# Low parts of the GLU gate's and output gate's weight slabs: by VectorE, or by ScalarE and an adding DMA

## The chip, the core and the metric

One core of a Trainium2 chip runs the whole kernel in one launch. The metric is the device time in microseconds (us); the kernel before and the kernel after are compared on the same chip. The engines are named as in the profile: PE is TensorE, DVE is VectorE, ACT is ScalarE, POOL is GpSimd, and SP is SyncE, whose queue issues most DMAs.

## The reference

A trunk of two pre-norm residual layers and a final RMSNorm, over 512 positions of width 1024, in float32. The change lies in the first (even) layer:

```python
def even_layer(x, norm_g, w_in, w_uq, q_g, w_ukv, kv_g, conv_w, conv_b, ln_g, ln_b, w_out, cos, sin):
    u = rms_norm(x, norm_g) @ w_in
    q_c, kv_c, k_r, z_b, glu_a, glu_g, z_a = jnp.split(
        u, _offsets(Q_LORA, KV_LORA, QK_ROPE, MLA_W, CONV_W, CONV_W, CONV_W), axis=-1)
    o_b = mla(q_c, kv_c, k_r, w_uq, q_g, w_ukv, kv_g, cos, sin) * jax.nn.silu(z_b)
    o_a = conformer_conv(glu_a, glu_g, conv_w, conv_b, ln_g, ln_b) * jax.nn.silu(z_a)
    return x + (jnp.concatenate([o_b, o_a], axis=-1) @ w_out).astype(x.dtype)
```

`mla` is attention with 16 heads over low-rank queries and keys. `conformer_conv` forms `a * sigmoid(g)` (the GLU), then a depthwise convolution of width 31, a LayerNorm and a swish. The second (odd) layer has a Mamba-2 mixer and a short convolution.

## The kernel before

**Products in two parts.** PE multiplies in float32r. To reach float32's accuracy every operand is split into a high part (rounded to float32r) and a low part (the rest), and a product is three: high by high, high by low, low by high. A weight matrix comes in slabs of up to 128x1024 (8 k-tiles by 128 output channels), each of which gives one 128x512 tile of the result in 24 matmuls: 16 that read the high part `w_hi`, then 8 that read the low part `w_lo` (`mm_cm`, line L325 of the profile).

**The slabs.** `Weights` holds the list of all slabs in the order of their use. `_prepare` does one slab: it loads it from DRAM into `w_raw` (line L87, issued on SP's queue), casts it to `w_hi` on ACT (L91), and makes `w_lo` in one of two ways. For slabs whose key is in `BY_DMA` (all of the odd layer, save one) ACT writes minus the slab, rounded to float32r, into `w_lo` (L93), and a DMA that POOL issues adds `w_raw` to it in place (L94). For all others one subtraction `w_raw - w_hi` does it (L96): on DVE if the key is in `EARLY`, else on POOL, and the slabs of the output projections alternate between the two. There are two `w_raw` buffers and three each of `w_hi` and `w_lo` (the odd layer gets one more now and then). `next(key)` first prepares slabs until one slab beyond the asked one is ready (three beyond, for keys in `BY_DMA`), then hands one out. A counter `self.i` is raised at the head of `_prepare`, after the slab's entry was read.

**The order of the work.** The program only states what depends on what; a list scheduler at build time, with the program's order as priority and its own costs, writes one fixed queue for each engine. Each engine then runs its queue in order.

**The attention's loop.** It has eight passes (p = 0 to 7), each of two heads. A pass makes scores and exponentials (`probs`: PE, then the row maximum on DVE at L538, the exponential on ACT at L540), writes the inverse sums to DRAM and reads them back broadcast (`inverse`, L550 and L554, on SP's queue), makes the next keys (`uk` slabs), then a tile of the GLU (slabs `a` and `g`; in the last two passes two `za` slabs stand there instead), transposes the probabilities (`turn`: PE, then copies `pt` on ACT and DVE at L563), makes the output gate (slab `zb`, L359 and L360), and weighs the values (`weigh`, L573). After p = 1, 3 and 5 it also makes the next queries and values (`up_proj`, slabs `uq` and `uv`, copies `q_tm` at L510). Two tiles of the GLU are made ahead of the loop, with two `a` and two `g` slabs.

**The convolution.** `conv31` stands after the loop in the program, and the scheduler spreads it over the loop as work of low priority: 22 taps on DVE (L488), 8 side taps on POOL (L483 to L486), then ACT copies DVE's sum (`cs`, L490) and POOL adds both (`u`, L491). There is one buffer for the side taps and one for `cs`.

The list's order in the loop, by key:

```python
    for p in range(8):
        out += ["uk"] * (p < 7)
        out += (["a", "g"] if p < 6 else ["za", "za"]) + ["zb"]
        if p % 2 and p < 7:
            out.append("up%d" % ((p + 1) // 2))
```

Counted from one, slab 16 is the `a` of p = 0, slab 17 the first `g` in the loop; the two `g` ahead of it are slabs 8 and 10. Each "up" is three slabs (two `uq` and a `uv`).

Of the kernel before, what the change touches and what calls it, by code (L numbers as in the profile page):

```python
# [66 lines left out]
BY_DMA = ("C", "B", "x", "zc", "h", "gc", "gb", "zd")  # L67
# [3 lines left out]
class Weights:  # L71
# [7 lines left out]
    def _prepare(self):  # L79
        nc = self.tc.nc  # L80
        key, ap, kt, n = self.slabs[self.i]
        eng = nc.vector if key in EARLY or key in ("oe", "oo") and self.i % 2 else nc.gpsimd
        self.i += 1
        more = key in BY_DMA and self.i % 3 == 0
        raw = (self.more if more else self.pool).tile([P, D], F32, name="w_raw", tag="w_raw",
                                                      bufs=1 if more else self.raw_bufs)[:, :kt * n]
        nc.sync.dma_start(raw, ap)  # L87
        more = key in BY_DMA and self.i % 4 == 0
        hi, lo = ((self.more if more else self.pool).tile([P, D], F32R, name=nm, tag=nm, bufs=1 if more else self.bufs)
                  [:, :kt * n] for nm in ("w_hi", "w_lo"))  # L90
        nc.scalar.copy(hi, raw)  # L91
        if key in BY_DMA:
            nc.scalar.mul(lo, raw, -1.0)  # L93
            nc.gpsimd.dma_start(lo, raw, accum_op=ALU.add)  # L94
        else:
            eng.tensor_tensor(lo, raw, hi.bitcast(F32), op=ALU.subtract)  # L96
        v = lambda t: t.rearrange("p (k n) -> p k n", k=kt)
        self.ready.append((key, v(hi), v(lo)))
# [1060 lines left out]
```

## Time and profile before

| | |
|---|---|
| median of 3 runs | 958.86 us (955.78 to 959.15) |
| the profiled execution | 958.48 us |
| its span, first to last instruction | 956.7 us |
| mean granted clock of TensorE | 0.992 |
| PE, weight loads, DVE, ACT, POOL busy | 920.2, 741.1, 696.0, 507.7, 310.1 us |
| low parts by L96 on DVE | 74 slabs, 83.0 us |
| low parts by L96 on POOL | 20 slabs, 47.7 us |
| low parts by L93 and L94 | 45 slabs, 47.5 us on ACT, 39.2 us on POOL |

A row of the profile's groups reads: line, engine, operation, what it writes and reads, the shape of the first form, the count, then the busy time in us, the mean time of one in ns, and the idle time of the engine just before them with what ended it. A row of the timeline has the start in us from the span's first instruction, the duration in us, the engine, the line and the operation, and in brackets the idle time before it and its releaser. A row of the stretches has the busy time of PE, weight loads, DVE, ACT and POOL with the number of instructions, then the granted clock, the DMA engines' share and their GB/s.

### The profile page before, as it was taken

What the parts mean: (1) busy time and instruction counts of PE and PEld (TensorE: products, weight loads), DVE (VectorE), ACT (ScalarE), POOL (GpSimd) and SP (SyncE); (2) the same over time, 40 slices, a digit from 0 to 9 for tenths busy, and PEclk for the clock granted to TensorE, in tenths of its full rate; (3) what the DMA queues carried; (4) which work ended last, traced back from release to release, by engine and by line L of the source; (5) the groups of instructions that cost most, each with busy time, mean ns of one, the idle gap of its engine ahead of it and who ended that gap; (6) DMA issues with size and microseconds to landing.
All of it is one profiled execution on the core that took longest, in us unless ns stands there. A gap on an engine that the chain in (4) does not pass through costs nothing.

```text
span 956.7 us, 12593 instructions
## 1 busy us (share of the span) xinstructions
PE 920.2 (96%) x4528; PEld 741.1 (77%) x4528; DVE 696.0 (73%) x1292; ACT 507.7 (53%) x964; POOL 310.1 (32%) x269
## 2 busy tenths in 40 slices
PE   7899998999999999999999899999999999999996
PEld 7888686776877677888889578878786886888885
DVE  4699888999988999893163779777866886466315
ACT  6645454544554444373135487777667757444322
POOL 0142716347073443283222121121212222234222
PEclk9999999999999999999999899999999999999998
DMA  8303302212122215423347679868676776732222
GB/s 317 106 28 112 57 22 95 60 51 86 45 70 83 66 56 97 132 92 111 96 161 201 158 211 220 195 157 214 163 196 159 215 170 161 196 113 74 88 81 88
DMA packets 48373, 119.57 MB, mean 125 GB/s; under 512 B 12808, under 2 KB 14472, under 8 KB 48312
## 3 DMA queue, kind: packets, MB, share of 16 engines
q1 hardware_dynamic: 35304, 82.61, 26.7%
q0 software_dynamic: 6480, 23.60, 13.7%
q10 hardware_dynamic: 6528, 12.58, 4.4%
q8 instruction: 35, 0.57, 0.2%
q14 instruction: 26, 0.21, 0.1%
HBM read 90.85 MB, written 4.33 MB: 99 GB/s over the span
## 4 chain that ended last, share of the span: by engine, by line
PE 79%; DVE 13%; DMA 3%; ACT 3%; issue 1%; POOL 0%; SPq 0%; DVEq 0%; ACTq 0%; POOLq 0%
PE acc L325 39%; PE acc L352 10%; PE tp L352 5%; PE sb L352 5%; PE sb L536 5%; PE tp L273 5%; PE acc L573 3%; PE cv L352 3%; PE cv L945 2%; PE tp L961 1%; DMA sums_d<-sums 1%; ACT w_hi L91 1%; PE sb L273 1%; DVE w_lo L96 1%; DMA w_raw<-in_w_cm_o 1%
## 5 line engine op out<-in xcount | busy, mean ns | idle before, releaser
L325 PE MATMUL acc<-xT_hi,w_hi 128*128 128x512 f32 x616 | 249.2, 406 | 2.7 <-ACT xT_hi L413 2.7
L325 PE MATMUL acc<-xT_lo,w_hi 128*128 128x512 f32 x616 | 246.7, 401 | 0.1
L91 ACT CAST w_hi<-w_raw 128x1024 fp32r<-128x1024 f32 (+7 forms) x139 | 134.8, 971 | 200.8 <-PE acc L325 85.6
L325 PE MATMUL acc<-xT_hi,w_lo 128*128 128x512 f32 x616 | 155.1, 391 | 0.0
L96 DVE TENSOR_TENSOR w_lo<-w_raw,w_hi 128x1024 fp32r<-128x1024 f32 (+6 forms) x74 | 83.0, 1121 | 88.2 <-ACT w_hi L91 77.6
L325 PEld LDWEIGHTS acc<-xT_hi,w_hi 128*128 128x128 f32 x616 | 116.9, 190 | 27.3 <-ACT xT_hi L413 2.9
L488 DVE SCALAR_TENSOR_TENSOR cv<-u,pc,cv 128x497 f32<-128x497 f32 (+10 forms) x176 | 130.2, 740 | 10.1 <-ACT cv L477 7.7
L325 PEld LDWEIGHTS acc<-xT_lo,w_hi 128*128 128x128 f32 x616 | 116.8, 190 | 24.5 <-POOL xT_lo L414 0.8
L325 PEld LDWEIGHTS acc<-xT_hi,w_lo 128*128 128x128 f32 x616 | 115.4, 188 | 24.1
L94 POOL DMA_DIRECT2D w_lo<-w_raw x45 | 39.2, 871 | 180.5 <-ACT w_lo L93 128.2
L96 POOL TENSOR_TENSOR w_lo<-w_raw,w_hi 128x1024 fp32r<-128x1024 f32 (+1 forms) x20 | 47.7, 2387 | 112.0 <-ACT w_hi L91 104.2
L486 POOL TENSOR_TENSOR side<-side 128x510 f32<-128x510 f32 (+3 forms) x56 | 78.6, 1403 | 4.7
L491 POOL TENSOR_TENSOR u<-cs,side 128x512 f32<-128x512 f32 x8 | 11.0, 1375 | 157.1 <-issue 149.9
L540 ACT ACTIVATE p<-sb,mx 128x512 f32<-128x512 f32 x64 | 43.4, 683 | 20.8 <-DVE mx L538 20.5
L485 POOL TENSOR_SCALAR side<-u,pc 128x510 f32<-128x510 f32 (+3 forms) x56 | 50.2, 897 | 4.7
L93 ACT ACTIVATE w_lo<-w_raw 128x1024 fp32r<-128x1024 f32 x45 | 47.5, 1056 | 2.2 <-PE acc L325 2.2
L928 DVE SCALAR_TENSOR_TENSOR e<-e,nacs 128x128 f32<-128x128 f32 x96 | 30.1, 347 | 22.6 <-ACT e L927 22.5
L538 DVE TENSOR_REDUCE mx<-sb 128x1 f32<-128x512 f32 x64 | 41.7, 685 | 3.2 <-PE sb L536 2.6
L923 DVE SCALAR_TENSOR_TENSOR f<-cbm,dt,f 128x128 f32<-128x128 f32 x96 | 39.2, 444 | 5.6 <-ACT f L922 5.6
L273 PEld LDWEIGHTS tp<-kc,p 128*128 128x128 f32 x256 | 28.9, 140 | 16.1 <-ACT pt L563 10.7
L728 DVE SCALAR_TENSOR_TENSOR c<-acc,pc,c 128x510 f32<-128x510 f32 (+1 forms) x48 | 35.8, 745 | 6.3 <-ACT c L726 5.7
L536 PE MATMUL sb<-k_t,qk_hi 128*128 128x512 f32 (+1 forms) x128 | 39.5, 403 | 0.4 <-DVE k_t L264 0.4
(325 smaller groups left out, 1836.8 us busy)
## 6 DMA issues: line engine op xcount, KB each, us to landing
w_raw<-in_w_cm_o SPq DMA_DIRECT2D x45, 512.0 KB, 4.8
w_lo<-w_raw POOLq DMA_DIRECT2D x45, 512.0 KB, 5.9
w_raw<-in_w_cm_e SPq DMA_DIRECT2D x32, 512.0 KB, 3.5
e<-acs ACTq DMA_DIRECT2D x24, 512.0 KB, 6.0
w_raw<-in_w_out_e SPq DMA_DIRECT2D x16, 512.0 KB, 3.5
w_raw<-in_w_out_o SPq DMA_DIRECT2D x16, 512.0 KB, 3.3
xt<-in_xT SPq DMA_DIRECT2D x8, 256.0 KB, 5.1
x_t<-in_x SPq DMA_DIRECT2D x4, 512.0 KB, 6.3
```

The costliest lines, as they stand in the source:

```text
L91: nc.scalar.copy(hi, raw)
L93: nc.scalar.mul(lo, raw, -1.0)
L96: eng.tensor_tensor(lo, raw, hi.bitcast(F32), op=ALU.subtract)
L273: T.transpose(tp[:rows, j * P:(j + 1) * P], b, ident)
L325: T.matmul(a, l, r, start=n == 0, stop=n == 3 * kk - 1)
L352: T.matmul(accs[t][:, :n], l, r, start=k1 == 0 and c == 0, stop=end and c == len(seq) - 1)
L485: G.tensor_scalar(t[:, o], ut[:, i], wt(j), 0.0, op0=ALU.mult, op1=ALU.add)
L486: G.tensor_tensor(side[:, o], side[:, o], t[:, o], op=ALU.add)
L488: V.scalar_tensor_tensor(c[:, o], ut[:, i], wt(j), c[:, o], op0=ALU.mult, op1=ALU.add)
L536: T.matmul(s, l[:, qs], r, start=n == 0, stop=n == 2)
L538: V.tensor_reduce(mx, s, axis=AX.X, op=ALU.max, negate=True)
L540: SC.activation(p, s, AF.Exp, bias=mx, accum_out=sums[:, q:q + 1])
```

## The change

From the 17th slab on, slabs with the keys `g` and `zb` get their low part as those in `BY_DMA` do: a multiplication by -1 on ACT and an adding DMA from POOL's queue, instead of a subtraction on DVE. The number of slabs prepared ahead is as it was, since `next` still goes by `BY_DMA` alone.

```diff
         nc.scalar.copy(hi, raw)
-        if key in BY_DMA:
+        if key in BY_DMA or key in ("g", "zb") and self.i > 16:
             nc.scalar.mul(lo, raw, -1.0)
             nc.gpsimd.dma_start(lo, raw, accum_op=ALU.add)
         else:
             eng.tensor_tensor(lo, raw, hi.bitcast(F32), op=ALU.subtract)
```

## The prediction

> **What bounds the kernel now.** I read the page first: its busy line, its chain, and the groups that the change touches.
>
> ```profile
> span 956.7 us, 12593 instructions
> PE 920.2 (96%) x4528; PEld 741.1 (77%) x4528; DVE 696.0 (73%) x1292; ACT 507.7 (53%) x964; POOL 310.1 (32%) x269
> PE 79%; DVE 13%; DMA 3%; ACT 3%; issue 1%; POOL 0%; SPq 0%; DVEq 0%; ACTq 0%; POOLq 0%
> L96 DVE TENSOR_TENSOR w_lo<-w_raw,w_hi 128x1024 fp32r<-128x1024 f32 (+6 forms) x74 | 83.0, 1121 | 88.2 <-ACT w_hi L91 77.6
> L93 ACT ACTIVATE w_lo<-w_raw 128x1024 fp32r<-128x1024 f32 x45 | 47.5, 1056 | 2.2 <-PE acc L325 2.2
> ```
>
> TensorE (PE) is busy for 96% of the span and holds 79% of the chain that ended last. Line L93, with the DMA that L94 issues, is the other way of making a low part, which 45 slabs of the odd layer already use: its prices stand in this trace. The attention's loop runs from about 84 to 380 us, so I asked for that window, and for what PE waited for in it (columns of the waits: us in total, times, longest).
>
> ```profile
> 84.00:380.00 296.00, 289.19 (x1422) 217.08 (x1421) 269.17 (x396) 143.31 (x290) 132.10 (x121) 1.00 0.25 66
> PE acc L352 <- ACT q_tm L510: 3.8, 3, 1.5
> PE acc L573 <- DVE pt L563: 1.8, 2, 0.9
> PE tp L273 <- DVE pt L563: 0.9, 1, 0.9
> PE tp L273 <- ACT pt L563: 0.2, 1, 0.2
> L488 DVE SCALAR_TENSOR_TENSOR cv<-u,pc,cv 128x501 f32<-128x501 f32 (+10 forms) x155 | 114.7, 740 | 9.7 <-ACT cv L477 7.7
> ```
>
> In order: PE 289.19 of 296 us, weight loads, VectorE (DVE) 269.17, ScalarE (ACT) 143.31, GpSimd (POOL) 132.10, the granted clock 1.00, the DMA engines a quarter busy. So DVE is 91% full and looks like a second bound, but PE is 98% full: it idles 296 - 289.2 = 6.8 us, of which the four waits name 3.8 + 1.8 + 0.9 + 0.2 = 6.7. None of them is for a `w_lo`. That is the ceiling of what any relief of DVE can return here. The biggest part of DVE's load, 114.7 us, is filler: the convolution's taps (L488), which nothing on PE needs before the loop is over.
>
> **The change, part by part.** The test `self.i > 16` comes after the increment, so slabs from the 17th on count: of the GLU gate six ("g" of p = 0 to 5; the two before the loop keep VectorE), of the output gate all eight ("zb"). That makes 14 slabs of 128x1024.
>
> (1) *Removed from DVE:* 14 subtractions. One takes 1.21 us in the row at 156.23 below (up to 1.64 at 229.08), 14 x 1.21 = 17 us at least; DVE's 269 becomes about 252. On the path this is worth only what PE waited for behind one of the 14. I looked at each PE gap and what DVE did just ahead.
>
> ```profile
> 150.19 0.39 PE L352 MATMUL acc<-w_hi,cT_hi 128*128 128x256 f32 x1 [1.50 <-ACT q_tm L510]
> 156.23 1.21 DVE L96 TENSOR_TENSOR w_lo<-w_raw,w_hi 128x1024 fp32r<-128x1024 f32 x1
> 157.70 0.68 DVE L563 COPY pt<-tp 128x512 f32<-128x512 f32 x1
> 158.43 1.07 PE L573 MATMUL acc<-pt,v_tm 128*64 128x512 f32 x2 [0.92 <-DVE pt L563]
> 227.20 1.05 ACT L91 CAST w_hi<-w_raw 128x1024 fp32r<-128x1024 f32 x1 [1.69 <-DMA w_raw<-in_w_cm_e]
> 228.15 0.48 ACT L510 ACTIVATE q_tm<-acc 128x384 f32<-128x384 f32 x1
> 229.08 1.64 DVE L96 TENSOR_TENSOR w_lo<-w_raw,w_hi 128x1024 fp32r<-128x1024 f32 x1
> 233.77 0.66 PE L273 MATMUL tp<-kc,p 128*128 128x128 f32 x4 [0.92 <-DVE pt L563]
> 311.60 1.21 DVE L96 TENSOR_TENSOR w_lo<-w_raw,w_hi 128x1024 fp32r<-128x1024 f32 x1
> ```
>
> The gap at 158.43 has a "g" (p = 2) subtraction right ahead of the late copy: that one can go, 0.9 us. The gap at 233.77 has an "a" slab's ahead of it (229.08), which stays on DVE; the same holds for the third of these gaps, near 314, where a "za" slab's stands ahead (311.60). The three waits for `q_tm` (the gap at 150.19 is one) are for ACT, which cast an "a" or "za" slab just ahead (227.20, itself late for its load, then the `q_tm` copy at 228.15); those casts stay. Bounds: 0 and -6.8; I take -1.0, nearest to the row of the one gap that has a moved subtraction ahead of it.
>
> (2) *Added to ACT:* 14 multiplications by -1 (L93) of 1.056 us, 14.8 us on an engine with 143 of 296 busy. They are ready as soon as the slab has landed and can stand in ACT's idle stretches, but ACT runs in order, and one of them can stand ahead of an exponential or a `pt` copy.
>
> ```profile
> L91 ACT CAST w_hi<-w_raw 128x1024 fp32r<-128x1024 f32 (+4 forms) x40 | 34.7, 868 | 42.2 <-PE acc L325 28.8 <-DVE mx L538 4.9 <-DMA w_raw<-in_w_cm_e 3.7
> ```
>
> Bounds: 0 (all in idle time) and +14.8 (each holds PE for its whole length). Nearer to 0, since PE waited 0.2 us for ACT's `pt` in the whole loop while 40 casts of about that length (L91) stood in the same queue, and 3.8 for `q_tm`: per such instruction 4.0 / 40 = 0.1 us, times 14 = 1.4. The `q_tm` part belongs to casts beside `up_proj`, where only two of the moved slabs ("g" of p = 2 and 4) stand, so I take a third of it, +0.5.
>
> (3) *Added to POOL:* 14 DMA issues.
>
> ```profile
> L94 POOL DMA_DIRECT2D w_lo<-w_raw x45: 852/862/1039, 511.4 to 834.0; - x45
> 100.34 1.95 POOL L491 TENSOR_TENSOR u<-cs,side 128x512 f32<-128x512 f32 x1 [22.29 <-issue]
> 118.00 1.29 POOL L486 TENSOR_TENSOR side<-side 128x508 f32<-128x508 f32 x1
> 139.31 1.30 POOL L491 TENSOR_TENSOR u<-cs,side 128x512 f32<-128x512 f32 x1 [20.02 <-issue]
> POOL u L491 <- issue: 149.9, 7, 25.1
> ```
>
> At 0.862 us each (median) they add 12.1 us to 132 of 296. A pass of POOL's work on the convolution runs from 100.34 (L491, then the side taps) to 119.3; then it waits for the taps of DVE until 139.31. It stood idle 149.9 us in seven such waits, so the issues cost POOL nothing: 0. Behind an issue stand only side taps; `u` is wanted after the loop. The danger is the reverse, an issue behind the waiting L491 (first rival).
>
> (4) *The low part comes later.* On the DVE way a "zb" slab (p = 1) was cast at 117.45, subtracted by 118.89 + 1.48 = 120.4, and PE first read its `w_lo` at 139.03.
>
> ```profile
> 82.18 1.05 ACT L91 CAST w_hi<-w_raw 128x1024 fp32r<-128x1024 f32 x1 [0.58 <-DMA w_raw<-in_w_cm_e]
> 86.63 1.23 DVE L96 TENSOR_TENSOR w_lo<-w_raw,w_hi 128x1024 fp32r<-128x1024 f32 x1
> 97.85 1.98 PE L325 MATMUL acc<-xT_hi,w_lo 128*128 128x512 f32 x8
> 117.45 1.05 ACT L91 CAST w_hi<-w_raw 128x1024 fp32r<-128x1024 f32 x1 [1.98 <-PE acc L325]
> 118.89 1.48 DVE L96 TENSOR_TENSOR w_lo<-w_raw,w_hi 128x1024 fp32r<-128x1024 f32 x1
> 139.03 1.98 PE L325 MATMUL acc<-xT_hi,w_lo 128*128 128x512 f32 x8
> w_lo<-w_raw POOLq DMA_DIRECT2D x45, 512.0 KB, 5.9
> DMA to landing us min/median/max: 4.5/5.9/10.1
> ```
>
> The new way is cast, multiplication 1.06, issue, landing 5.9 from the issue (10.1 at the worst): 118.5 + 1.06 + about 1 for an exponential let through + 5.9 = 126.5, and 131 at the worst. It fits with 8 to 12 us to spare. The tightest is the loop's first "g": subtraction done at 87.9, PE reads at 97.85, 10.0 us spare; its cast ends early (83.2), so the sum lands it near 91 or 95. The other casts stand two slabs ahead of PE as well, because a cast waits for the third-last slab to leave its buffers. Cost 0, with that cover; without it the worst landing costs 10.1 - 5.9 = 4.2 us a slab.
>
> (5) *The raw buffer is held longer.* There are two `w_raw`, and the load of slab n+2 on SP waits for the low part of slab n. It now waits for a landing.
>
> ```profile
> 164.53 1.22 DVE L96 TENSOR_TENSOR w_lo<-w_raw,w_hi 128x1024 fp32r<-128x1024 f32 x1
> 165.77 7.00 SPq L87 DMA_DIRECT2D w_raw<-in_w_cm_e  x2
> 176.97 1.06 ACT L91 CAST w_hi<-w_raw 128x1024 fp32r<-128x1024 f32 x1 [0.68 <-PE acc L325]
> w_raw<-in_w_cm_e SPq DMA_DIRECT2D x26, 512.0 KB, 3.6
> sums_d<-sums SPq DMA_DIRECT2D x8, 4.0 KB, 10.6
> ```
>
> Behind the "zb" of p = 2 the next "a" was loaded at 165.77 and cast at 176.97. Now the load starts near 164.5 + 1.1 + 0.6 + 5.9 = 172.1 (where the subtraction stood, multiplication, wait for an exponential, landing) and is there at 175.7: 1.3 us before the cast. SP is in order: the 4 KB of `sums` and their two reads (`inv`) queue behind the load, and `inv` is wanted only in the next pass. Cost 0 at the median landing; if the landing takes 10.1, the cast starts 2.9 us late with ACT's exponentials and `pt` copies behind it (second rival).
>
> (6) *DMA traffic:* 14 x 512 KB more in a stretch with the DMA engines at 0.25; 14 x 5.9 = 83 us of transfer, at other moments than most loads. 0, the contention being in the 10.1 above.
>
> Sum: -1.0 + 0.5 = -0.5 us. The profiled execution took 958.48 us (span 956.7 and 1.8 around it), 0.4 below the median of 958.86: 958.48 - 0.5 = **958.0**, no change that can be measured. About 0.5% (4.8 us: below 954.1 or above 963.6) is what tells this kernel from no change.
>
> One rule of the Trainium skill speaks against the change. Ahead of it, the rows: the 45 issues of L94 (part 3) take 0.85 to 1.04 us, in a stretch in which DVE was busy for 257 of 360 us.
>
> ```profile
> 500.00:860.00 360.00, 347.83 (x1753) 285.05 (x1752) 256.91 (x562) 237.04 (x456) 80.33 (x79) 0.99 0.72 184
> ```
>
> The page "SBUF — State Buffer" (section "SBUF: two separate sides") says that a DMA issued from GpSimd needs descriptors written through the port pair that VectorE can lock, so that one of 620 ns alone took 3100 ns beside a VectorE copy. By that rule each of the 14 would be some 2.5 us later (an estimate from that page) in a loop with DVE at 91%; the rows do not show it, with DVE at 71%.
>
> As a mechanism of this kernel, in its own rows: an issue held for one or two DVE instructions (1.2 to 1.6 us) eats the 1.3 us of part (5); at some six slabs with so little to spare that is 6 x 0.5 = 3 us, 961.
>
> **The rivals.** *A: an issue queued behind L491.* Where the queue, written at build time, has the multiplication's DMA behind the `u` of the convolution, it goes out at 139.31 + 1.30 instead of 120, lands at 140.6 + 5.9 = 146.5, and PE, which wants it at 139.03, stalls 7.5 us. Against it: the issue is ready near 120 and L491 only 19 us later, so an order by readiness is plain. It decides from one such "zb" (p = 1, 2 and 4 have the pattern): 958 + 7.5 = 965.5, with all three 980. Chance 0.07.
>
> *B: late raw loads hold ACT.* Landings near 10.1 instead of 5.9 delay casts by 2.9 us at some three slabs, with PE's `pt` and exponentials behind them: up to 8.7, PE loses most of it, 958 + 7 = 965. For: landings of 10.1 occur, and the write of `sums` takes 10.6 us for 4 KB. Against: DMA at 0.25 here and 0.72 where 10.1 was seen. Chance 0.10. It decides from about 3 us of lateness at two slabs.
>
> *C: DVE was the real pace.* With 17 us off, the copies and splits that PE waits for come earlier everywhere, and the whole 6.8 us of gaps close: 958.5 - 6.8 = 951.7. For: DVE at 91%. Against: two of the three DVE gaps have unmoved work ahead. Chance 0.14.
>
> *D: the port rule* above, 961, chance 0.06.
>
> **How the numbers follow.** My forecast has 0.63, D 0.06: "same" 0.69. C gives "faster" 0.14. A and B give "slower" 0.17. The range goes to C below (952) and past B and one case of A above (966); outside lie A with more than one slab and the far part of C, some 0.1 to 0.15.
>
> **What would show it.** L96 on DVE falls from 74 to 60, L93 and L94 rise from 45 to 59. In the window of the loop DVE falls to about 252, ACT rises to 158, POOL to 144, PE stays near 289 and the loop ends within 3 us of 380. No wait of PE for a `w_lo` DMA appears; the DVE wait ahead of the 158 gap is gone, the ones near 233 and 314 stay. SP waits for the `w_lo` DMA in the loop where it waited for L96. A PE wait for `w_lo`, or an ACT cast that waits for `w_raw` for over 3 us, would make the prediction wrong, as would PE gaps of under 3 us in all; so would a different order on PE after the loop.

## The result, and the profile after

The changed kernel takes 964.99 us (median of 9 runs, 961.07 to 967.64) against 958.86 (955.78 to 960.38): 1.0061 of before, 95% interval 1.0046 to 1.0076. It is slower by about 6 us. The profiled execution took 961.70 us, one of the quickest of the nine and 3.2 us above the profiled one before (958.48), so its trace can show only about half of the 6 us. Its page:

```profile
span 959.9 us, 12641 instructions
PE 919.7 (96%) x4528; PEld 737.9 (77%) x4528; DVE 681.1 (71%) x1278; ACT 520.6 (54%) x978; POOL 312.7 (33%) x283
PE 72%; DVE 16%; DMA 4%; POOL 3%; ACT 3%; issue 2%; SPq 0%; DVEq 0%; ACTq 0%; POOLq 0%
L94 POOL DMA_DIRECT2D w_lo<-w_raw x59 | 51.4, 870 | 276.3 <-ACT w_lo L93 207.7
L96 DVE TENSOR_TENSOR w_lo<-w_raw,w_hi 128x1024 fp32r<-128x1024 f32 (+6 forms) x60 | 66.9, 1115 | 93.9 <-ACT w_hi L91 82.8
L93 ACT ACTIVATE w_lo<-w_raw 128x1024 fp32r<-128x1024 f32 x59 | 62.4, 1058 | 2.3 <-PE acc L325 2.3
```

The work moved as stated: L96 on DVE from 74 to 60, L93 and L94 from 45 to 59. PE's share of the chain fell from 79% to 72%; POOL, at 0% before, now has 3%, and DVE 16% instead of 13%. The loop's window, then the waits of PE in the loop and those of ACT's casts for a load (us in total, times, longest):

```profile
84.00:380.00 296.00, 285.50 (x1401) 213.47 (x1400) 254.78 (x382) 153.18 (x301) 133.33 (x134) 1.00 0.36 90
```

```profile
PE tp L273 <- ACT pt L563: 4.5, 2, 3.2
PE tp L273 <- DVE pt L563: 4.3, 6, 1.4
PE acc L352 <- ACT q_tm L510: 0.9, 1, 0.9
PE sb L536 <- DVE qk_lo L264: 0.4, 1, 0.4
ACT w_hi L91 <- DMA w_raw<-in_w_cm_e: 15.5, 7, 5.6
ACT w_hi L91 <- DMA w_raw<-in_w_uq: 3.8, 1, 3.8
```

PE idles 296 - 285.5 = 10.5 us where it idled 6.8. The waits for `q_tm` fell from 3.8 to 0.9, so part of the old ceiling was returned, but two waits for ACT's `pt`, 4.5 us in all, took its place, and those for DVE's copies rose from 2.7 to 4.3. From the first product of the scores (L536, at 79.97 us; 81.66 before) to the first product behind the last `weigh` (L325, at 383.15; 379.90 before) PE took 303.2 us instead of 298.2.

The larger of the two waits for ACT can be followed link by link. These rows of the timeline of after stand in order of time (start, duration, engine, line; in brackets the idle time and what ended it); rows between them are left out:

```profile
241.52 0.70 POOL L485 TENSOR_SCALAR side<-u,pc 128x510 f32<-128x510 f32 x1
242.50 1.05 ACT L93 ACTIVATE w_lo<-w_raw 128x1024 fp32r<-128x1024 f32 x1
...
248.81 1.28 POOL L486 TENSOR_TENSOR side<-side 128x508 f32<-128x508 f32 x1
250.02 0.89 POOL L94 DMA_DIRECT2D w_lo<-w_raw  x1
254.67 0.80 SPq L87 DMA_DIRECT2D w_raw<-in_w_cm_e  x2
258.32 1.04 ACT L91 CAST w_hi<-w_raw 128x1024 fp32r<-128x1024 f32 x1 [5.59 <-DMA w_raw<-in_w_cm_e]
259.27 0.59 ACT L466 ACTIVATE u<-acc 128x512 f32<-128x512 f32 x1
259.76 0.58 ACT L563 COPY pt<-tp 128x512 f32<-128x512 f32 x1
260.39 0.66 PE L273 MATMUL tp<-kc,p 128*128 128x128 f32 x4 [3.18 <-ACT pt L563]
```

The product for the "zb" slab of p = 4 is done at 243.55. Its DMA should go out then, but in POOL's fixed queue it stands behind the convolution's side taps, of which one goes on to 250.09, and starts at 250.02, 6.5 us late. It lands 4.6 us later, and SP's load starts at once, at 254.67; only then is the raw buffer free for the "a" slab of p = 5, which in the kernel before was loaded 10.4 us earlier:

```profile
244.24 7.23 SPq L87 DMA_DIRECT2D w_raw<-in_w_cm_e  x2
```

ACT runs in order. The cast of that slab, not urgent in itself, waits 5.59 us for the load, and a `pt` copy that PE does want stands behind it. The same happens to the "zb" of p = 5: issue 6.2 us late at 285.84, cast 3.80 us late, PE waits 1.3 us near 294. A third cast, of the "g" of p = 1, waits over 3 us too, and for another reason:

```profile
106.21 1.05 ACT L91 CAST w_hi<-w_raw 128x1024 fp32r<-128x1024 f32 x1 [5.35 <-DMA w_raw<-in_w_cm_e]
```

Here the issue that holds the buffer was in time (91.24). The load waited for its landing, went out at 96.53, and took 9.6 us beside the write of `sums` (issued at 97.58, 9.3 us); the median 128x1024 load of the loop took 4.4. The timeline has no wait of PE between 102.00 and 153.83, so this cast cost it nothing.

Why POOL was busy with taps at that moment is seen in the convolution. DVE's taps (L488), before and after:

```profile
L488 DVE SCALAR_TENSOR_TENSOR cv<-u,pc,cv x159: 723/741/751, 87.8 to 384.5; 128x501 f32<-128x501 f32 x15, 128x500 f32<-128x500 f32 x15, 128x499 f32<-128x499 f32 x15, 128x498 f32<-128x498 f32 x15
```

```profile
L488 DVE SCALAR_TENSOR_TENSOR cv<-u,pc,cv x159: 723/742/752, 84.9 to 349.2; 128x501 f32<-128x501 f32 x15, 128x500 f32<-128x500 f32 x15, 128x499 f32<-128x499 f32 x15, 128x498 f32<-128x498 f32 x15
```

The last one of the loop starts at 349.2 instead of 384.5. DVE's freed time went to this filler. POOL's side taps of a tile can start once the tile before is finished, so they moved forward too: a pass of them ran at 221 to 240 and the next at 264 to 282 before, and runs at 236 to 253 now, across the moment at which the issue is ready.

### The profile page after: what moved, and what is told of

Read it like the earlier page. It is cut to its first block, busy times and chain, and to the rows that moved or that the text cites. A ratio compares the mean times of both kernels' runs of the same rounds, so it can differ in the third digit from the quotient of the medians.

```text
span 959.9 us, 12641 instructions
## 1 busy us (share of the span) xinstructions
PE 919.7 (96%) x4528; PEld 737.9 (77%) x4528; DVE 681.1 (71%) x1278; ACT 520.6 (54%) x978; POOL 312.7 (33%) x283
## 4 chain that ended last, share of the span: by engine, by line
PE 72%; DVE 16%; DMA 4%; POOL 3%; ACT 3%; issue 2%; SPq 0%; DVEq 0%; ACTq 0%; POOLq 0%
PE acc L325 34%; PE acc L352 9%; PE tp L352 5%; PE sb L352 5%; PE tp L273 4%; PE sb L536 4%; PE acc L573 3%; PE cv L352 3%; PE cv L945 2%; DVE cv L488 2%; DVE w_lo L96 2%; POOL side L486 1%; DMA w_raw<-in_w_cm_o 1%; PE tp L961 1%; DMA w_lo<-w_raw 1%
## 5 line engine op out<-in xcount | busy, mean ns | idle before, releaser
L325 PE MATMUL acc<-xT_hi,w_hi 128*128 128x512 f32 x616 | 248.4, 404 | 2.7 <-ACT xT_hi L413 2.7
L325 PE MATMUL acc<-xT_lo,w_hi 128*128 128x512 f32 x616 | 246.4, 401 | 0.4 <-POOL xT_lo L414 0.4
L325 PE MATMUL acc<-xT_hi,w_lo 128*128 128x512 f32 x616 | 155.1, 391 | 0.0
L94 POOL DMA_DIRECT2D w_lo<-w_raw x59 | 51.4, 870 | 276.3 <-ACT w_lo L93 207.7
L325 PEld LDWEIGHTS acc<-xT_hi,w_hi 128*128 128x128 f32 x616 | 116.5, 189 | 27.1 <-ACT xT_hi L413 2.9
L325 PEld LDWEIGHTS acc<-xT_lo,w_hi 128*128 128x128 f32 x616 | 116.6, 189 | 25.0 <-POOL xT_lo L414 0.8
L488 DVE SCALAR_TENSOR_TENSOR cv<-u,pc,cv 128x497 f32<-128x497 f32 (+10 forms) x176 | 130.4, 741 | 5.4 <-ACT cv L477 2.3
L325 PEld LDWEIGHTS acc<-xT_hi,w_lo 128*128 128x128 f32 x616 | 115.4, 188 | 24.1
L96 DVE TENSOR_TENSOR w_lo<-w_raw,w_hi 128x1024 fp32r<-128x1024 f32 (+6 forms) x60 | 66.9, 1115 | 93.9 <-ACT w_hi L91 82.8
L96 POOL TENSOR_TENSOR w_lo<-w_raw,w_hi 128x1024 fp32r<-128x1024 f32 (+1 forms) x20 | 47.7, 2387 | 120.9 <-ACT w_hi L91 103.1
L486 POOL TENSOR_TENSOR side<-side 128x510 f32<-128x510 f32 (+3 forms) x56 | 73.9, 1320 | 4.7
L93 ACT ACTIVATE w_lo<-w_raw 128x1024 fp32r<-128x1024 f32 x59 | 62.4, 1058 | 2.3 <-PE acc L325 2.3
L485 POOL TENSOR_SCALAR side<-u,pc 128x510 f32<-128x510 f32 (+3 forms) x56 | 46.5, 830 | 4.5
L273 PE MATMUL tp<-kc,p 128*128 128x128 f32 x256 | 36.7, 278 | 9.1 <-ACT pt L563 4.5
L536 PE MATMUL sb<-k_t,qk_hi 128*128 128x512 f32 (+1 forms) x128 | 40.0, 405 | 0.4 <-DVE k_t L264 0.4
```

What stands on the lines that cost most here:

```text
L273: T.transpose(tp[:rows, j * P:(j + 1) * P], b, ident)
L325: T.matmul(a, l, r, start=n == 0, stop=n == 3 * kk - 1)
L485: G.tensor_scalar(t[:, o], ut[:, i], wt(j), 0.0, op0=ALU.mult, op1=ALU.add)
L486: G.tensor_tensor(side[:, o], side[:, o], t[:, o], op=ALU.add)
L488: V.scalar_tensor_tensor(c[:, o], ut[:, i], wt(j), c[:, o], op0=ALU.mult, op1=ALU.add)
L536: T.matmul(s, l[:, qs], r, start=n == 0, stop=n == 2)
```

## The experiments

The theory was the chain above: late issue in POOL's queue, raw buffer held, late load, ACT's cast in front of `pt`. The rivals: ACT's 14 products; the DMA traffic; subtractions that stay on DVE and take longer beside POOL. Kernels of one series ran on one chip and share the runs of the kernel before, whose medians were 957.28, 958.67, 959.46 and 958.15 us in the four series.

| series, kernel | median us | ratio to before | 95% interval |
|---|---|---|---|
| 1 the changed kernel again | 964.50 | 1.0072 | 1.0055 to 1.0089 |
| 1 added from DRAM | 960.19 | 1.0028 | 1.0016 to 1.0040 |
| 1 all but two slabs | 959.79 | 1.0027 | 1.0016 to 1.0038 |
| 1 VectorE's relief alone | 958.19 | 1.0000 | 0.9981 to 1.0020 |
| 2 products, no DMA | 961.05 | 1.0023 | 1.0008 to 1.0038 |
| 2 changed, no side taps | 951.55 | 0.9930 | 0.9907 to 0.9953 |
| 2 before, no side taps | 953.78 | 0.9958 | 0.9941 to 0.9975 |
| 2 GLU gate alone | 960.40 | 1.0015 | 1.0001 to 1.0030 |
| 3 the two slabs alone | 959.96 | 1.0006 | 0.9991 to 1.0020 |
| 3 products twice | 963.73 | 1.0051 | 1.0033 to 1.0069 |
| 3 relief alone, once more | 962.04 | 1.0026 | 1.0009 to 1.0044 |
| 4 relief alone (no product) | 959.93 | 1.0023 | 1.0009 to 1.0038 |
| 4 one product | 960.11 | 1.0030 | 1.0010 to 1.0049 |
| 4 three products | 958.84 | 1.0009 | 0.9992 to 1.0025 |

**The changed kernel again.** No edit.

> The changed kernel once more, unchanged, to have it beside the three below and to see whether its time goes with the granted clock. Every theory: 965 us, 1.006 of before. The first theory (an issue that is late in POOL's fixed queue holds a raw buffer, the load after it is late, and ACT's cast of that slab holds up copies of pt) expects TensorE to wait some 3 us for ACT near 260 us and some 1.3 us near 294, as in the profile of the changed kernel, and the clock to stand below 0.99 in the executions above 964 us. The rival, that nothing hangs on these two waits, expects nothing of them.

The loss is there again, with the same two waits (4.6 us, the longest 3.3), and the clock behaved as expected: the executions up to 963.9 us had a mean granted clock of 0.989 to 0.992, those from 965.1 us on 0.987. This profile caught a stretch at half clock. PE in its timeline (rows left out between those shown), then the same two microseconds in the windows of after and of this run (PE, weight loads, DVE, ACT, POOL, granted clock, DMA share):

```profile
257.56 0.40 PE L325 MATMUL acc<-xT_lo,w_hi 128*128 128x512 f32 x1
261.30 1.11 PE L273 MATMUL tp<-kc,p 128*128 128x128 f32 x4 [3.35 <-ACT pt L563]
262.07 0.78 PE L325 MATMUL acc<-xT_hi,w_hi 128*128 128x512 f32 x1
262.64 0.63 PE L325 MATMUL acc<-xT_lo,w_hi 128*128 128x512 f32 x1
264.94 0.40 PE L325 MATMUL acc<-xT_hi,w_hi 128*128 128x512 f32 x1
```

```profile
262.00:264.00 2.00, 2.00 (x12) 1.70 (x11) 1.97 (x4) 0.00 (x0) 0.00 (x0) 1.00 0.06 8
```

```profile
262.00:264.00 2.00, 2.00 (x7) 1.51 (x7) 1.39 (x3) 0.59 (x1) 0.00 (x0) 0.50 0.00 0
```

After the wait TensorE runs at half its clock until about 264.1: 7 matmuls in a stretch that held 12, so 5/12 of 2 us, 0.8 us, are lost in this stretch alone. From the end of the wait to the first matmul that reads `w_lo` PE takes 5.5 us here (261.30 to 266.80) and 4.2 in the first profile (260.39 to 264.55), so 1.3 us are lost in all. In the first profile a wait of 3.18 us left the clock at 1.00. So the wait costs its own length, and in one of the two profiled executions a slow stretch on top; the executions from 965.1 us on were not profiled, and whether this is all that sets them apart is not shown. The Trainium skill, page "TensorE: Matmul & The Clock Gate", section "What's actually happening", has the clock fall after at least one idle window of about 3.4 us, in windows that run freely; by that rule no wait that is shorter should do it. The 3.18 us agree. The 3.35 us do not decide by their length alone, but the granted clock of the microsecond from 260 to 261 is already 0.86, which puts the fall some 2.8 us into the wait, too early for that rule; the measurement decides.

**Added from DRAM.** The DMA adds the slab from DRAM, so the raw buffer is free after ACT's product although the issue is as late as before.

```diff
-            nc.gpsimd.dma_start(lo, raw, accum_op=ALU.add)
+            nc.gpsimd.dma_start(lo, raw if key in BY_DMA else ap, accum_op=ALU.add)
```

> As the changed kernel, but the adding DMA of the 14 moved slabs reads the slab from DRAM a second time, not the raw buffer, so that the buffer is free after ACT's product and not after the landing. The first theory (late issue, raw buffer held, late load, ACT's cast) expects the two waits of TensorE for ACT near 260 and 294 us to be gone (3.2 + 1.3 us), no wait of the loads for a w_lo in the loop, and 960 to 961 us, 1.000 to 1.002 of before. Rival 1, that ACT's 14 products of 1.06 us are what costs: no gain, 965 us. Rival 2, that the added DMA traffic costs: not under 965 us, since the slabs are read twice from DRAM here. Rival 3, that it is the subtractions which stay on VectorE and take longer beside POOL: waits for DVE's copies of pt stay as they are, 965 us.

960.19 us, as expected, though the ratio of 1.0028 lies above the 1.002: 0.0044 of the 0.0072 is gone. The same place in its timeline:

```profile
250.78 0.89 POOL L94 DMA_DIRECT2D w_lo<-in_w_cm_e  x1
244.33 7.14 SPq L87 DMA_DIRECT2D w_raw<-in_w_cm_e  x2
254.85 1.05 ACT L91 CAST w_hi<-w_raw 128x1024 fp32r<-128x1024 f32 x1 [1.39 <-PE acc L325]
257.17 0.58 ACT L563 COPY pt<-tp 128x512 f32<-128x512 f32 x1
```

The issue is still late (250.78), yet the load goes out at 244.33, as in the kernel before, and the cast no longer waits for it. What SP waited for, in after and here:

```profile
SPq L87 <- DMA w_lo<-w_raw: 130.5, 14, 16.1
```

```profile
SPq L87 <- ACT w_lo L93: 58.5, 10, 10.0
```

The 14 waits for a landing are gone, and no PE wait for ACT's `pt` is left. More traffic (DMA share 0.39 in the loop against 0.36) did not hurt, which speaks against the second rival, and the waits for DVE's `pt` stayed (5.0 us, six times), so they are not what these 4.3 us were.

**All but two slabs.** The two late "zb" stay on DVE.

```diff
-        if key in BY_DMA or key in ("g", "zb") and self.i > 16:
+        if key in BY_DMA or key in ("g", "zb") and self.i > 16 and self.i not in (40, 44):
```

> As the changed kernel, but the low parts of two of the 14 slabs, the output gate's in the fifth and sixth part of the loop, are made by VectorE as before. These are the two whose issue stands behind the convolution's taps in POOL's queue by 6.5 and 6.2 us in the profile of the changed kernel. The first theory expects both waits for ACT to be gone and 960.5 us, 1.000 to 1.003 of before. Rivals 1 to 3 (ACT's products, DMA traffic, longer subtractions beside POOL) expect twelve fourteenths of the loss to stay: about 964 us, 1.005.

959.79 us. Two slabs of 14 carry 0.0045 of the 0.0072, as the chain says and not two fourteenths. The 0.0027 that remain are at the upper edge of what I expected; the later runs look for their cause.

**The two slabs alone**, the converse: `key in BY_DMA or self.i in (40, 44)`.

> As the kernel before, but two of the 14 slabs are moved: the output gate's in the fifth and sixth part of the loop, the two that the kernel with twelve moved leaves out. Both issues stand behind all taps of a tile in POOL's queue. The first theory (late issue, buffer held, late load, ACT's cast) expects the waits of TensorE for ACT of some 3 and 1.3 us here too, and 3 to 5 us lost: 961 to 963 us, 1.003 to 1.005, about as much as the other twelve cost or more. If what is lost goes with the number of moved slabs: two fourteenths of 0.6%, 1.001.

A miss for my expectation: 1.0006, no loss. The POOL rows of its timeline say why:

```profile
238.72 1.27 POOL L486 TENSOR_TENSOR side<-side 128x508 f32<-128x508 f32 x1
245.70 1.04 POOL L94 DMA_DIRECT2D w_lo<-w_raw  x1 [5.71 <-ACT w_lo L93]
```

The issue still stands behind a tile's taps, but with twelve subtractions back on DVE the convolution is not ahead, the taps end at 240, and POOL waits 5.71 us for the product instead of the reverse. The lateness is made by the other twelve: relief of DVE, convolution ahead, taps in the way. The raw buffer is held until the landing here too, and the load of the next "a" goes out about 6 us later than the 244.24 of the kernel before:

```profile
250.41 1.44 SPq L87 DMA_DIRECT2D w_raw<-in_w_cm_e  x2
```

Yet its cast, at 255.94, does not wait for it (255.73 in the kernel before). With the issue in time, holding the buffer costs nothing at this place.

**No side taps**, in the changed kernel and in the kernel before: seven of POOL's eight taps are left out, one stays.

```diff
         for n, j in enumerate(SIDE):
             o, i = taps.pop(j)
+            if n > 0:
+                continue
```

> As the changed kernel, but of the eight taps of the 31-tap convolution that POOL computes only the first is (seven taps are left out, 14 instructions for each of eight tiles): the issues of the adding DMA no longer stand behind taps in POOL's queue, and VectorE's subtractions no longer run beside them. To be read against the next kernel, in which the same taps are left out of the kernel before. The first theory (late issue in POOL's queue, buffer held, late load, ACT's cast) expects no wait of the casts for a slab near 258 and 293 us, and at most 0.3% between the two. If ACT's products or the DMA traffic made the loss, it stays whole: 0.6 to 0.7% between the two.

> As the kernel before, with the same seven taps of eight left out on POOL. All theories: 955 to 958 us, 0.997 to 1.001 of before, since POOL has room in the loop in the kernel before (132 us busy of 296).

Without the taps the change does not lose: 0.9930 against 0.9958, the one over the other 0.997 (0.994 to 1.000, from the two intervals taken as independent). The kernel before gains 0.4% by it, where I expected 0.3% at most. No cast waits for a slab near 258 or 293. One does at another place, the one that is late at 106.21 in the changed kernel: its load went out at 96.81, when the adding DMA ahead of it had landed, and took 10.7 us beside the write of `sums` (issued at 97.67, 10.2 us). It costs PE 1.6 us:

```profile
107.61 1.04 ACT L91 CAST w_hi<-w_raw 128x1024 fp32r<-128x1024 f32 x1 [6.50 <-DMA w_raw<-in_w_cm_e]
```

**VectorE's relief alone.** Nothing takes the place of the 14 subtractions; the high part is read for the low one.

```diff
+        if key in ("g", "zb") and self.i > 16:
+            lo = hi
-        if key in BY_DMA:
+        elif key in BY_DMA:
```

> The kernel before, without any low part for the 14 slabs (the products that read the low part read the high part instead, so TensorE's work is the same): VectorE is relieved of 14 subtractions of 1.21 us and nothing else is loaded. It is what the change could bring at most. The first theory expects a small gain, 1 to 3 us: 956 to 958 us. The rival that VectorE is the pace in the loop expects up to 6.8 us of TensorE's idle time in the loop back, 952 us. Should it be slower than before, the order on the other engines, not a load, decides.

> The kernel with VectorE relieved of the 14 subtractions and nothing put in their place, once more, beside these two: 0.998 to 1.002 of before if the relief is worth nothing in the loop, as in the first series; under 0.997 if that series hid a gain.

1.0000, 1.0026 and, in the fourth series, 1.0023: no gain in any, and the gain of 1 to 3 us that the first theory expected did not come. So in the kernel with its taps no gain of this change can be seen even where nothing takes the subtractions' place, and the convolution, which runs ahead, is off the path. The three intervals overlap, so a difference between the chips is not shown. The waits of PE in the run of 1.0026:

```profile
PE acc L354 <- ACT q_tm L512: 6.9, 3, 2.4
ACT w_hi L91 <- DMA w_raw<-in_w_cm_e: 6.3, 3, 2.8
```

The waits for `q_tm` were there before with 3.8 us. They too are a cast of a late slab in front of a copy that PE wants.

**ACT's products.** The changed kernel without the adding DMA of the 14 slabs, with each product made once, twice or three times; and the slabs of the GLU gate alone.

```diff
             nc.scalar.mul(lo, raw, -1.0)
-            nc.gpsimd.dma_start(lo, raw, accum_op=ALU.add)
+            if key in BY_DMA:
+                nc.gpsimd.dma_start(lo, raw, accum_op=ALU.add)
```

> As the changed kernel, but without the adding DMA of the 14 slabs: ACT makes the 14 products and nothing is added to them (the low parts are wrong; that part of the computation is left out). VectorE is relieved, ACT is loaded, POOL issues nothing more, and the raw buffer comes free after ACT's product. With the buffer freed early 2.5 us of the loss stay (959.8 to 960.2 us, 1.0027). If these come from ACT's 14 products of 1.06 us, which lie ahead of ACT's copies, this kernel shows them too: 959.5 to 960 us, 1.002 to 1.003. If they come from what the 14 issues do on POOL's queue, or from the DMA traffic, it stands at 957 to 958 us, 1.000, as the kernel with VectorE relieved alone.

> As the changed kernel, but only the GLU gate's 7 slabs are moved; the output gate's 7 stay on VectorE. None of the two issues that came 6.5 and 6.2 us late is among them. The first theory expects no wait of ACT's casts for a slab and at most half of the 2.5 us that stayed: 957.5 to 959 us, 1.000 to 1.0015. If each moved slab costs alike, half of 7 us: 960.8 us, 1.0035.

> As the kernel with the 14 products and no adding DMA for them, but ACT makes each of the 14 products twice (28 of 1.06 us; the low parts are wrong, that part of the computation is left out). If it is ACT's load that costs the 0.23% there, twice the load costs 0.4 to 0.5%: 961.5 to 963 us. If ACT has the room that my prediction gave it (about 0.5 us for 14) and the 0.23% are of another cause, it stays at 1.002 to 1.003.

Once 1.0023, twice 1.0051, which looked like ACT's load; but the two stood on different chips. Relief alone, on the chip of the 1.0051, had 1.0026; the intervals overlap, and PE waits less for ACT's `q_tm` with the products made twice (5.7 us) than without any (6.9). The GLU gate alone (six slabs, not the seven named above: L94 stands 51 times instead of 45) gave 1.0015, at the upper edge of the theory's guess, with no long wait of a cast for a slab. So the number of products was varied on one chip:

> First of three on one chip with the 14 subtractions taken from VectorE, here with no product on ACT in their place (no low part is made for the 14 slabs; the products read the high part). If ACT's products are what stays of the loss once the buffer is freed early: 1.000 of before here, and the three in a line. If the relief of VectorE is what costs (its convolution taps run ahead and stand ahead of copies, as in the second series of this kernel): 1.002 to 1.003 here already.

> Second of the three: one product on ACT for each of the 14 slabs, no adding DMA (the low parts are wrong; the addition is left out). If ACT's products cost, 0.2 to 0.3% above the kernel without products; if the relief costs, as that kernel.

> Third of the three: three products on ACT for each of the 14 slabs (42 of 1.06 us, 44.5 us in all; the addition is left out). If ACT's time costs in proportion: 0.6 to 0.9% above the kernel without products, 1.007 to 1.010 of before. If ACT's idle time hides them: within 0.2% of the kernel with one product.

The loop's window with no, one and three products (ACT is the fourth of the engines):

```profile
84.00:380.00 296.00, 289.04 (x1424) 216.51 (x1423) 255.40 (x387) 143.05 (x293) 123.26 (x122) 1.00 0.22 66
```

```profile
84.00:380.00 296.00, 288.62 (x1417) 215.16 (x1416) 255.84 (x385) 155.85 (x306) 123.28 (x122) 1.00 0.22 67
```

```profile
84.00:380.00 296.00, 291.31 (x1421) 216.34 (x1420) 254.05 (x387) 182.69 (x335) 122.76 (x123) 1.00 0.22 68
```

ACT's load rises by 40 us and PE does not lose: 1.0023, 1.0030, 1.0009. So on this chip ACT's idle time hides the products, and the first rival falls for the 0.0044, which went while all 14 products stayed (added from DRAM). What makes up the 1.0051 of the products made twice is open. For the other 0.0027 the cause is not shown: in series 3 and 4 an offset of that size is there with the relief alone, without product or DMA, but in series 1, where the 0.0027 and 0.0028 were measured, relief alone had 1.0000 (0.9981 to 1.0020). Each edit is also scheduled anew, so the kernels differ in the order of their queues as well, and what that alone is worth was not measured. In which rows the 0.0027 lies I could not settle.

## Why the prediction was wrong, by its own steps

- *Step 5 failed.* It put the cost of the raw buffer's longer hold at 0, with 1.3 us to spare, from "multiplication, wait for an exponential, landing". The sum had no term for the issue's wait on POOL. With 6.5 us of it the load came 10.4 us later than before and the cast 5.59 us late. In place of the 0 the runs show 0.0044 to 0.0045, 4.3 us, gone when the buffer is freed early or the two slabs are left out. The hold itself was not the mistake: in the kernel with the two slabs alone one issue is in time and the other 3.5 us late, and neither cast waits for its load. The other 0.0027, 2.6 us, stays open.
- *Step 3 is where the missing term belongs.* It asked what stands behind an issue (side taps, rightly unimportant) and named an issue behind the waiting L491 as the danger. It did not ask what stands ahead of an issue, and it read POOL's idle times from a trace in which DVE was not yet relieved.
- *Step 1 was of the wrong size and sign.* The gap at 158.43 went, as said, and DVE's load came out at 254.8 for the 252 forecast; two of the three waits for `q_tm`, which were to stay, went too; but in place of the gain of 1.0 us relief alone brought none (1.0000) or a loss (1.0023 and 1.0026). What DVE saves goes to the convolution. Two of the six waits for DVE's `pt` in the profile after (0.84 and 1.36 us) come right behind an "a" subtraction that stays and now runs beside POOL's taps; the first of them took 1.23 us before, with no wait behind it, and now:

```profile
99.03 2.31 DVE L96 TENSOR_TENSOR w_lo<-w_raw,w_hi 128x1024 fp32r<-128x1024 f32 x1
101.27 0.68 DVE L563 COPY pt<-tp 128x512 f32<-128x512 f32 x1
```

- *Steps 2, 4 and 6 held, as far as the runs tell.* ACT rose to 153.2 (158 forecast) at no cost that three products could show; the products made twice leave that a little open. PE waited for no `w_lo`; the landings in the loop had a median of 4.8 us and 8.4 at the worst. The DMA share rose to 0.36, and 0.39 with the slabs added from DRAM was not slower.
- *Rival B was the right link with the wrong cause.* It had late loads hold ACT, priced 965 and let it decide from 3 us at two slabs; there were three such casts, of 5.35, 5.59 and 3.80 us. But it made slow landings the reason and got 0.10 for that. Only the first was a slow load, and that one cost PE nothing here; behind the two that count, the issue was late and its landing took 4.6 and 4.9 us. That 964.99 us were measured is luck: the 7 us were three casts of 2.9, while the runs give 4.3 us to two casts and leave the rest without a shown cause. Rival A had the right queue and the wrong instruction in it. Rival C falls by the relief runs, none of which is faster. Rival D's late issues are not seen: the 14 issues took 0.85 to 1.04 us in a loop with DVE at 86%. The sign that was to make the prediction wrong, a cast over 3 us late for `w_raw`, is the one that came.

## What to carry to other kernels

When a step moves to an in-order queue, ask what stands ahead of it there at the moment it is ready, in the new schedule: relieving one engine lets filler run ahead, and the filler's partner on another engine can then stand in front of the step. Where a step that frees a buffer becomes a DMA, follow the buffer: next load, the instruction that waits for the load, and what is queued behind that one. If the relieved engine only gains time for filler, there is nothing to win; leaving the work out, as here, shows that before anything is built in its place.

## What the runs showed of the hardware

- A wait of TensorE of about 3 us may or may not halve its clock: 3.18 us did not, 3.35 did. In the kernel with one product and no DMA (second series) 2.62 us did; its PE row and the windows around it (granted clock third from the end, 1.00, 0.59, 0.56):

```profile
232.29 0.55 PE L353 MATMUL acc<-w_hi,cT_hi 128*128 128x256 f32 x1 [2.62 <-ACT q_tm L511]
```

```profile
230.00:232.00 2.00, 0.00 (x0) 0.00 (x0) 0.00 (x0) 1.20 (x2) 0.00 (x0) 1.00 0.61 234
232.00:234.00 2.00, 1.71 (x8) 1.71 (x9) 1.73 (x4) 0.83 (x4) 0.00 (x0) 0.59 0.09 31
234.00:236.00 2.00, 2.00 (x12) 2.00 (x12) 1.21 (x3) 1.09 (x3) 0.00 (x0) 0.56 0.42 131
```

  The rule of a whole idle window, cited above, does not cover this one, which is clearly shorter than the window. Why one wait does it and a longer one does not is open.
- A subtraction of 128x1024 on VectorE takes 1.22 us on average in the loop of the changed kernel without seven of POOL's eight side taps (12 subtractions) and 1.37 with all of them (12), up to 2.31 in the row at 99.03 above; in the kernel before it is 1.22 (26) against 1.35 (27). The Trainium skill, page "SBUF — State Buffer", section "Who interferes with whom", says that an operation of VectorE on two tensors in SBUF contends with GpSimd's reads; the averages agree with it.
